# A hybrid decoder block on one core: four changes of issue order, placement and pacing in the input projection and at the start of attention

## Chip, cores and metric

The kernel runs on one core of one Trainium2 chip. The metric is the device time of one execution in microseconds (us); the time of a kernel is the median of its runs.

## The reference

One decoder block on x of 1024 tokens by 1024 channels, in float32:

```
hn   = rmsnorm(x, norm_mix)
proj = hn @ w_in          # fq fk fv ff | gq gk gv ga gb gz | gate_fox gate_gdn
y_fox = softmax(fq fk^T / sqrt(128) + cumulated log f, causal) fv        # 8 heads of 128
q, k, v = silu(causal conv of gq, gk, gv);  q, k l2-normalised
S_t = exp(g_t) (I - b_t k_t k_t^T) S_{t-1} + b_t k_t v_t^T;  o_t = S_t^T q_t   # gated delta rule
y_gdn = rmsnorm(o) * silu(gz)
h  = x + (sigmoid(gate_fox) * (y_fox @ w_branch_fox) + sigmoid(gate_gdn) * (y_gdn @ w_branch_gdn)) @ w_out
up = causal conv of (rmsnorm(h, norm_ffn) @ w_up)
out = rmsnorm(h + (silu(up_gate) * up_val) @ w_down, norm_final)
```

## The kernel before

Every float32 operand of a large product is split into a rounded high part (a cast on ScalarE, `split`, L103) and the low rest (a subtraction on VectorE or GpSimd); a product is then three matmuls: high by high, high by low, low by high. The instructions of TensorE stand in the order in which the program writes them. Those of the other engines and of the SP queue, which issues the transfers, are ordered by a scheduler that estimates when each is ready. `keep_in_program_order` pins an instruction behind the one that the program wrote before it on the same engine; later ones may still be put ahead of it.

The stages that the change touches:

**head_in (L554), 0 to about 127 us.** Tokens come in eight row tiles. For each, `norm_rows` normalises it, `columns` transposes it on TensorE and splits it into the blocks 11, 21, 12 and 22 (two halves of the channels by two halves of the tokens), and `rows` multiplies a row tile with a group of token-major weights: 24 gate columns and the values, four groups (`wgroup`, L567). A group comes as four quarters through a ring `vwr` of three raw tiles; each quarter is cast (`vwh`) and subtracted (`vwl`). Group 0 runs beside the columns, one tile behind them; groups 1 to 3 follow. Between group 0 and group 1 the program writes seven small parameter loads (`parameters`, L521, all pinned), and the low parts of group 1 are pinned on VectorE. At the start TensorE multiplies ones fifteen times (L620), with results that nobody reads. During groups 1 and 2 `block_sums` (L341) builds the blocks t1 to t4, sums and differences of the four. `scalars` (L664) computes decays from the gate columns and the parameters.

**project (L745), to about 816 us.** All other columns of w_in, 40 pairs of 128, by Strassen's scheme with seven products per pair of chunks: each product is twelve matmuls (`block_product`), and within a job the blocks come in the order 21, t2, t3, t1, (11 of the next job), 22, t4. Raw weights come through a ring `wr` of three tiles; operands are prepared three ahead (`lookahead`). The variable `left` counts the matmuls that are left. Side work is taken in steps between them: sums of the branch weights, the convolutions, the inverse of the chunk matrices on VectorE, then `prepare_lead` (L1051; a step whenever left is a multiple of 20), which stores split weights for a later stage, then `fox_first` (L1120), which loads the first attention head (ql, kl, cr, vl) and splits query and key. The last sixteen chunks are the gates: `gate(e)` (L786) takes the Tanh on ScalarE (pinned) and stores the chunk (L793) from the SP queue.

**mix (L1241), to about 1076 us.** Attention of eight heads (`fox`, L1211), 26 steps for each, with two interleaved scans of the delta rule (`stream`, `scan`). A scan's inputs are loaded by `prep(h)` (L1252), all pinned on SP: sat, sx (twice), sxt, svt, skT, skt, saq, sqd. While the second half of a head is attended, the next head's query (step 0) and key (step 3) are split by casts pinned on ScalarE (L1100) and subtractions on GpSimd.

Memory is reused by pools: a tile waits until the tiles that lay there are done. The scan's tiles lie where the blocks and the weights of project lay.

Of the kernel before, what the change touches and what calls it, by code (L numbers as in the profile page):

```python
# [9 lines left out]
F32 = mybir.dt.float32  # L10
# [7 lines left out]
P = 128  # L18
# [3 lines left out]
NT = S // P  # L22
# [45 lines left out]
def finish(gen):  # L68
    for _ in gen:
        pass  # L70
# [17 lines left out]
class Block:  # L88
# [322 lines left out]
    def run(self):  # L411
# [5 lines left out]
        with ExitStack() as ctx:  # L417
# [16 lines left out]
            banks(8)  # L434
            blk = self.blocks(pool(right, "hn", side="right"), ("11", "21", "22"))
            self.st = pool(right, "stream", side="right")
# [117 lines left out]
    def head_in(self, blk, right):  # L554
# [3 lines left out]
        with tc.tile_pool(name="hin", bufs=1) as pool, ExitStack() as px:  # L558
# [7 lines left out]

            def wgroup(g, eng):  # L567
                wh = pool.tile([P, KD * VGW], F32R, tag="vwh", bufs=2, name="vwh")
                wl = pool.tile([P, KD * VGW], F32R, tag="vwl", bufs=2, name="vwl")
                for q in range(4):  # L570
                    sl = slice(q * 2 * VGW, (q + 1) * 2 * VGW)
                    wr = pool.tile([P, 2 * VGW], F32, tag="vwr", bufs=3, name="vwr")
                    nc.sync.dma_start(wr, a["w_tok"][g][:, sl])
                    nc.scalar.copy(wh[:, sl], wr)
                    low = eng.tensor_tensor(wl[:, sl], wr, wh[:, sl].bitcast(F32), ALU.subtract)
                    if g == 1:

                        tc.keep_in_program_order(low)
                return wh, wl

# [37 lines left out]

            ps = self.small()
            for _ in range(15):  # L620
                nc.tensor.matmul(ps[:, 0:P], self.ones, self.ones, start=True, stop=True)
            xs = []
# [10 lines left out]
            for t in range(NT):  # L633
                xn = self.norm_rows(xs[t], xp, "x")
                if t == 0:
                    w0 = wgroup(0, nc.vector)
                if t + 2 < NT:
                    xload()
                columns(xn, t)
                if t:  # L640
                    rows(0, t - 1, *w0)
            rows(0, NT - 1, *w0)
            finish(params)
            px.close()
            blk.update(self.blocks(right.enter_context(tc.tile_pool(name="hnt", bufs=1, side="right", reuse_waits="tile")),
                                   ("t1", "t2", "t3", "t4")))
            scalars = self.scalars()
            for g in range(1, NVG):
                w = wgroup(g, nc.vector if g == 1 else nc.gpsimd)
                take(scalars, 1)  # L650
                for t in range(NT):
                    rows(g, t, *w)
                    if (g, t) == (2, 0):

                        self.pin = True
                        self.early = [self.wload(a["w_gdn"][i * H]) for i in range(2)]
                        self.pin = False
                    if t % 4 == 2 and g < 3:
                        sl = slice((2 * (g - 1) + t // 4) * P, (2 * (g - 1) + t // 4 + 1) * P)
                        self.block_sums(blk, whole("12", sl), whole("22", sl), sl, pool, pin=True)  # L660
# [84 lines left out]
    def project(self, blk, fox_pool):  # L745
# [40 lines left out]
        def gate(e):  # L786
            def gen(_, c):
                for _ in range(3):
                    yield
                for sl in halves[::-1]:  # L790

                    tc.keep_in_program_order(nc.scalar.activation(c[:, sl], c[:, sl], AF.Tanh, scale=0.5))
                nc.sync.dma_start(self.gt_d[e], c)  # L793
                yield
# [115 lines left out]
        with ExitStack() as ix:  # L910
            for i, _ in enumerate(self.strassen(jobs, blk, pace=3)):
# [32 lines left out]
                elif fox is None:  # L944
                    if left % 20 == 0 and not take(prep, 1):
                        ix.close()
                        ws.close()
                        fox = self.fox_first(fox_pool())
                        take(fox, 1)
                elif left in (192, 168) or left < 120 and left % 12 == 0:  # L950
                    take(fox, 1)
# [259 lines left out]
    def fox(self, pools, scan_pool):  # L1211
# [6 lines left out]
        for h in range(H):  # L1218
# [5 lines left out]
            for half in range(2):  # L1224
                for i, _ in enumerate(self.attend(h, half, pts)):
# [5 lines left out]
                    elif h + 1 < H:  # L1231
                        if i == 0:
                            self.fox_query()
                        elif i == 3:
                            self.fox_key()
# [5 lines left out]
    def mix(self, fp, pool, before_last):  # L1241
        tc, nc, a = self.tc, self.nc, self.a
        self.yf_d, self.yg_d = ([self.dr.tile([P, S], F32, name=f"{n}{h}") for h in range(H)] for n in ("yfd", "ygd"))
        if True:
# [6 lines left out]

            def prep(h):  # L1252
                def ld(tag, src, bufs=3):
                    t = pool.tile([P, NB, P], F32, tag=tag, bufs=bufs, name=tag)
                    load(t, view(src))
                    return t
                at = pool.tile([Q, NB, Q], F32, tag="sat", bufs=1, name="sat")
                load(at, self.a21_d[h])
                x11 = pool.tile([Q, NB, Q], F32, tag="sx1", bufs=1, name="sx1")
                load(x11, self.x_d[:, h * NB:(h + 1) * NB])  # L1260
                x22 = pool.tile([Q, NB, Q], F32, tag="sx2", bufs=1, name="sx2")
                y22 = self.y_d[:, Q + h * NB:Q + (h + 1) * NB]
                load(x22, y22)
                xt = pool.tile([P, NB, P], F32, tag="sxt", bufs=3, name="sxt")
                nc.gpsimd.memset(xt[Q:P, :, 0:Q], 0.0)
                load(xt[0:Q, :, 0:Q], self.y_d[:, h * NB:(h + 1) * NB])
                load(xt[Q:P, :, Q:P], y22)
                vb = ld("svt", self.vt_d[h])
# [739 lines left out]
```

## Time and profile before

| | |
|---|---|
| median of 3 runs | 2010.86 us (2009.41 to 2011.02) |
| the profiled execution | 2003.4 us, its span 2001.7 us |
| TensorE busy | 1920.6 us (96%) |
| VectorE busy | 1485.8 us (74%) |
| ScalarE busy | 1069.3 us (53%) |
| GpSimd busy | 956.5 us (48%) |
| granted TensorE clock, mean | 0.989 |

The profile names the engines PE (TensorE), DVE (VectorE), ACT (ScalarE), POOL (GpSimd) and SPq (the SP queue, which issues transfers). Times are microseconds from the start of the span. In a timeline a row has its start, its length, the engine, the line of the code, the operation, what it writes and reads, and how many instructions are merged; in brackets stands the idle time before it with the instruction that ended it. A wait for several semaphores is put down to the one that came last by the profile.

### The profile page before, as it was taken

How to read it: one execution, taken by the hardware profiler on the slowest of the kernel's cores; microseconds unless marked ns; L12 is line 12 of the kernel's file. 1: busy time of each engine (PE TensorE's matmuls, PEld its weight loads, DVE VectorE, ACT ScalarE, POOL GpSimd, SP SyncE). 2: the span in 40 equal slices, each digit the busy share in tenths (PEclk: the TensorE clock that was granted, in tenths of full speed). 3: DMA queues.
4: the chain of work that ended last, by engine and by line, in shares of the span. 5: the costliest groups of instructions: out<-in, count | busy, mean ns of one | idle time of the engine just before them, and what ended most of it. 6: DMA issues, size and time to landing. Idle time of an engine off the chain costs nothing. (4 is left out here: it accounts for less than half of the span.)

```text
span 2001.7 us, 29195 instructions
## 1 busy us (share of the span) xinstructions
PE 1920.6 (96%) x9658; PEld 1606.0 (80%) x9658; DVE 1485.8 (74%) x2549; ACT 1069.3 (53%) x2383; POOL 956.5 (48%) x792
## 2 busy tenths in 40 slices
PE   8999999999999999899998999999999999999998
PEld 8988888888887887688886887877788888878886
DVE  6848888866999974487877797668877776768435
ACT  5336777763334445476666454476555555553234
POOL 2845655655545555455655043154665656630012
PEclk9999999999999999899999999999999999999999
DMA  4324655566333366766656643573433434378654
GB/s 146 97 97 162 196 182 188 173 210 210 119 108 110 112 223 244 243 225 205 236 188 231 223 150 133 179 244 130 163 122 115 146 118 137 125 246 311 212 195 158
DMA packets 191608, 350.89 MB, mean 175 GB/s; under 512 B 50784, under 2 KB 79712, under 8 KB 191456
## 3 DMA queue, kind: packets, MB, share of 16 engines
q1 hardware_dynamic: 191312, 348.50, 51.8%
q8 instruction: 76, 1.25, 0.3%
q14 instruction: 76, 0.62, 0.1%
q10 hardware_dynamic: 144, 0.52, 0.1%
HBM read 232.76 MB, written 116.20 MB: 174 GB/s over the span
## 5 line engine op out<-in xcount | busy, mean ns | idle before, releaser
L107 POOL TENSOR_TENSOR ol<-ws,oh 128x512 fp32r<-128x512 f32 x212 | 291.2, 1376 | 217.3 <-ACT oh L106 210.9
L107 POOL TENSOR_TENSOR ol<-wr,oh 128x512 fp32r<-128x512 f32 x165 | 230.8, 1401 | 272.4 <-ACT oh L106 222.3
L106 ACT CAST oh<-ws 128x512 fp32r<-128x512 f32 x212 | 131.1, 618 | 180.6 <-PE mm L159 172.9
L205 DVE TENSOR_TENSOR ws<-wr 128x512 f32<-128x512 f32 x106 | 105.2, 992 | 103.6 <-DMA wr<-in_w_up_dram 74.3
L106 ACT CAST oh<-wr 128x512 fp32r<-128x512 f32 x201 | 121.5, 615 | 111.1 <-PE mm L159 73.5
L390 DVE SCALAR_TENSOR_TENSOR cv<-c,fw,cv 128x512 f32<-128x512 f32 (+2 forms) x176 | 127.5, 748 | 11.0 <-ACT cv L385 9.3
L390 DVE SCALAR_TENSOR_TENSOR cv<-c,cw,cv 128x511 f32<-128x511 f32 (+2 forms) x144 | 105.9, 748 | 7.4 <-ACT cv L385 5.8
L1003 DVE TENSOR_TENSOR invt<-invz 128x399 f32<-128x399 f32 (+50 forms) x114 | 94.9, 847 | 0.3
L264 ACT COPY x<-mm 128x512 f32<-128x512 f32 x158 | 91.9, 581 | 4.5 <-PE mm L159 4.5
L159 PE MATMUL mm<-b22h,oh 128*128 128x512 f32 x216 | 85.9, 398 | 5.2 <-ACT x L264 4.8
L107 DVE TENSOR_TENSOR ol<-wd,oh 128x512 fp32r<-128x512 f32 x66 | 46.4, 706 | 58.7 <-ACT oh L106 58.7
L159 PE MATMUL mm<-bt4h,oh 128*128 128x512 f32 x216 | 85.3, 395 | 3.3 <-DVE c L311 3.3
L159 PE MATMUL mm<-bt1h,oh 128*128 128x512 f32 x216 | 85.0, 393 | 3.4 <-ACT x L264 3.3
L159 PE MATMUL mm<-b11h,oh 128*128 128x512 f32 x216 | 85.5, 396 | 1.0 <-ACT oh L106 1.0
L159 PE MATMUL mm<-bt4l,oh 128*128 128x512 f32 x216 | 86.2, 399 | 0.0
L159 PE MATMUL mm<-b22l,oh 128*128 128x512 f32 x216 | 86.0, 398 | 0.0
L159 PE MATMUL mm<-b21l,oh 128*128 128x512 f32 x216 | 86.0, 398 | 0.0
L159 PE MATMUL mm<-b11h,ol 128*128 128x512 f32 x216 | 85.3, 395 | 0.7 <-POOL ol L107 0.7
L159 PE MATMUL mm<-b11l,oh 128*128 128x512 f32 x216 | 85.7, 397 | 0.0
L159 PE MATMUL mm<-bt2l,oh 128*128 128x512 f32 x216 | 85.2, 394 | 0.3 <-DVE bt2l L107 0.3
L159 PE MATMUL mm<-bt2h,oh 128*128 128x512 f32 x216 | 84.5, 391 | 1.0 <-ACT x L264 1.0
L159 PE MATMUL mm<-bt1l,oh 128*128 128x512 f32 x216 | 84.9, 393 | 0.0
(426 smaller groups left out, 6372.2 us busy)
## 6 DMA issues: line engine op xcount, KB each, us to landing
wr<-in_w_up_dram SPq DMA_DIRECT2D x43, 512.0 KB, 3.6
wr<-in_w_gdn_dram SPq DMA_DIRECT2D x24, 512.0 KB, 3.7
wr<-in_w_out_dram SPq DMA_DIRECT2D x24, 512.0 KB, 3.5
s<-hy SPq DMA_DIRECT2D x44, 256.0 KB, 3.1
s<-z SPq DMA_DIRECT2D x44, 256.0 KB, 3.3
wd<-in_w_down_dram SPq DMA_DIRECT2D x44, 256.0 KB, 5.4
b22h<-s SPq DMA_DIRECT2D x44, 256.0 KB, 3.0
b22l<-s SPq DMA_DIRECT2D x44, 256.0 KB, 3.4
```

The costliest lines, as they stand in the source:

```text
L106: cast = nc.scalar.copy(hi, src)
L107: (lo_eng or nc.vector).tensor_tensor(lo, src, hi.bitcast(F32), ALU.subtract)
L159: self.nc.tensor.matmul(ps, lhs[:, sl], rhs[:, k, :], start=(first and k == 0 and i == 0), stop=(k == 3 and i == 2), skip_group_check=True)
L205: v.tensor_tensor(t, x, y, op)
L264: nc.scalar.copy(t, x)
L390: nc.vector.scalar_tensor_tensor(t[:, lo:], c[:, 512 * j + lo - s:512 * (j + 1) - s], w[:, n - 1 - s:n - s], t[:, lo:], op0=ALU.mult, op1= ...
L1003: nc.vector.tensor_tensor(tv, z[:, m:n, 0:n].to_broadcast([P, r, n]), z[:, m, c0:c1].unsqueeze(2).to_broadcast([P, r, n]), ALU.mult))
```

## The change

Gate stores from e = 10 on are issued from ScalarE's queue. `prep(0)` no longer pins its loads; those of later heads stay pinned. The block t4 moves from the pool "hnt" into the pool "hn", and the others are placed in the order t2, t3, t1. `wgroup` becomes a generator: the ring has four raw tiles, group 0 takes its last quarter after the first `columns` (pinned), and group 1's loads and casts are written after row tile 5 of group 0, pinned, with the parameters behind them; its low parts stay where they were. Eight more products of ones follow the first `columns`. The steps of `prepare_lead` come at multiples of 16, the first query and key are split at 180 and 156 matmuls left, and within a head the next query and key are split one step later (1 and 4).

```diff
-            blk = self.blocks(pool(right, "hn", side="right"), ("11", "21", "22"))
+            blk = self.blocks(pool(right, "hn", side="right"), ("11", "21", "22", "t4"))
...
             def wgroup(g, eng):
...
-                for q in range(4):
-                    sl = slice(q * 2 * VGW, (q + 1) * 2 * VGW)
-                    wr = pool.tile([P, 2 * VGW], F32, tag="vwr", bufs=3, name="vwr")
-                    nc.sync.dma_start(wr, a["w_tok"][g][:, sl])
-                    nc.scalar.copy(wh[:, sl], wr)
-                    low = eng.tensor_tensor(wl[:, sl], wr, wh[:, sl].bitcast(F32), ALU.subtract)
-                    if g == 1:
-                        tc.keep_in_program_order(low)
-                return wh, wl
+                raw, cuts = [], [slice(q * 2 * VGW, (q + 1) * 2 * VGW) for q in range(4)]
+                def high(q, pin):
+                    raw.append(pool.tile([P, 2 * VGW], F32, tag="vwr", bufs=4, name="vwr"))
+                    load = nc.sync.dma_start(raw[q], a["w_tok"][g][:, cuts[q]])
+                    cast = nc.scalar.copy(wh[:, cuts[q]], raw[q])
+                    if pin:
+                        tc.keep_in_program_order(load)
+                        tc.keep_in_program_order(cast)
+                def low(q, pin):
+                    ins = eng.tensor_tensor(wl[:, cuts[q]], raw[q], wh[:, cuts[q]].bitcast(F32), ALU.subtract)
+                    if pin:
+                        tc.keep_in_program_order(ins)
+                for q in range(3 if g == 0 else 4):
+                    high(q, g == 1)
+                    if g == 0:
+                        low(q, False)
+                yield wh, wl
+                if g == 0:
+                    high(3, True)
+                    low(3, False)
+                else:
+                    for q in range(4):
+                        low(q, g == 1)
...
-            ps = self.small()
-            for _ in range(15):
-                nc.tensor.matmul(ps[:, 0:P], self.ones, self.ones, start=True, stop=True)
+            def warm(n):
+                ps = self.small()
+                for _ in range(n):
+                    nc.tensor.matmul(ps[:, 0:P], self.ones, self.ones, start=True, stop=True)
+            warm(15)
...
                 if t == 0:
-                    w0 = wgroup(0, nc.vector)
+                    group = wgroup(0, nc.vector)
+                    w0 = next(group)
                 if t + 2 < NT:
                     xload()
                 columns(xn, t)
                 if t:
                     rows(0, t - 1, *w0)
+                else:
+                    finish(group)
+                    warm(8)
+                if t == NT - 2:
+                    group = wgroup(1, nc.vector)
+                    w1 = next(group)
+                    finish(params)
             rows(0, NT - 1, *w0)
-            finish(params)
             px.close()
             blk.update(self.blocks(right.enter_context(tc.tile_pool(name="hnt", bufs=1, side="right", reuse_waits="tile")),
-                                   ("t1", "t2", "t3", "t4")))
+                                   ("t2", "t3", "t1")))
             scalars = self.scalars()
             for g in range(1, NVG):
-                w = wgroup(g, nc.vector if g == 1 else nc.gpsimd)
+                if g > 1:
+                    group = wgroup(g, nc.gpsimd)
+                    w1 = next(group)
+                w = w1
+                finish(group)
                 take(scalars, 1)
...
-                nc.sync.dma_start(self.gt_d[e], c)
+                (nc.scalar if e >= 10 else nc.sync).dma_start(self.gt_d[e], c)
...
-                    if left % 20 == 0 and not take(prep, 1):
+                    if left % 16 == 0 and not take(prep, 1):
...
-                elif left in (192, 168) or left < 120 and left % 12 == 0:
+                elif left in (180, 156) or left < 120 and left % 12 == 0:
...
-                        if i == 0:
+                        if i == 1:
                             self.fox_query()
-                        elif i == 3:
+                        elif i == 4:
                             self.fox_key()
...
             def prep(h):
+                def load_input(dst, src):
+                    if h:
+                        load(dst, src)
+                    else:
+                        nc.sync.dma_start(dst, src)
...
-                    load(t, view(src))
+                    load_input(t, view(src))
...
-                load(at, self.a21_d[h])
+                load_input(at, self.a21_d[h])
...
```

The loads of x11, x22 and xt change in the same way.

## Rows read from the trace of the kernel before

**Rows 1.** Timeline of TensorE in head_in: dummy products and three waits.

```profile
1.19 5.49 PE L621 MATMUL ms<-ones 128*128 128x128 f32 x30 [1.19 <-POOL ones L509]
...
10.42 1.10 PE L605 MATMUL ms<-ident,nxn 128*128 128x128 f32 x8 [1.99 <-DVE nxn L551]
...
53.85 0.59 PE L587 MATMUL ms<-vwh,b21h 128*128 128x262 f32 x1 [5.95 <-ACT vwh L574]
...
105.34 0.39 PE L588 MATMUL ms<-vwl,b21h 128*128 128x262 f32 x1 [0.70 <-POOL vwl L575]
```

**Rows 2.** Timelines of ScalarE, SP and VectorE at the border of groups 0 and 1.

```profile
37.77 0.37 ACT L591 COPY vev<-ms 128x262 f32<-128x262 f32 x1
...
45.09 0.43 SPq L526 DMA_DIRECT2D nf<-in_norm_ffn_dram  x1
...
48.47 7.86 SPq L573 DMA_DIRECT2D vwr<-in_w_tok_dram  x5
...
49.11 0.31 DVE L686 SCALAR_TENSOR_TENSOR z<-sm,fb 128x64 f32<-128x64 f32 x1 [1.68 <-DMA fb<-in_fox_f_bias_dram]
```

**Rows 3.** Stretches at a lowered clock: length, busy of PE, PEld, DVE, ACT, POOL; clock, DMA, GB/s.

```profile
12.85:19.09 6.24, 6.24 (x30) 6.24 (x31) 5.39 (x10) 3.73 (x8) 1.89 (x3) 0.52 0.88 277
53.85:59.81 5.96, 5.52 (x23) 5.22 (x24) 5.82 (x9) 3.04 (x6) 3.31 (x3) 0.50 0.52 146
...
786.73:790.25 3.52, 3.52 (x10) 2.86 (x10) 0.90 (x5) 0.49 (x2) 2.23 (x2) 0.52 0.03 5
820.00:829.00 9.00, 6.84 (x50) 5.52 (x49) 7.85 (x25) 4.95 (x12) 1.89 (x3) 0.81 1.06 348
838.36:843.00 4.64, 4.64 (x30) 3.90 (x31) 2.53 (x5) 3.11 (x8) 4.30 (x5) 0.67 1.09 319
```

**Rows 4.** Timeline of TensorE, 780 to 840: its four waits of over 1 us.

```profile
784.17 0.38 PE L1152 MATMUL ms<-kh,qh 128*128 128x256 f32 x1 [1.54 <-ACT kh L1100]
786.73 0.54 PE L1153 MATMUL ms<-kl,qh 128*128 128x256 f32 x1 [2.17 <-POOL kl L1101]
...
823.45 1.19 PE L1283 MATMUL ms<-sx,sat 64*64 64x64 f32 x16 [2.16 <-DVE mm L1167]
...
838.36 0.79 PE L1316 MATMUL us<-su,saq 128*128 128x128 f32 x2 [6.76 <-DMA sx<-yd]
```

**Rows 5.** SP queue: longest wait in 770 to 816 (total, times, longest); three issues.

```profile
SPq L793 <- ACT c L792: 29.9, 5, 22.0
...
773.69 0.42 SPq L1084 DMA_DIRECT2D ql<-qd  x1
...
815.45 0.50 SPq L1250 DMA_DIRECT2D sat<-a21d  x1
...
825.94 0.32 SPq L1084 DMA_DIRECT2D ql<-qd  x1
```

**Rows 6.** Timeline of ScalarE at 837.

```profile
837.00 1.14 ACT L1100 CAST qh<-ql 128x512 fp32r<-128x512 f32 x2 [5.83 <-DMA ql<-qd]
838.05 0.26 ACT L1311 COPY su<-us 128x128 f32<-128x128 f32 x1
```

**Rows 7.** Three stretches around the start of attention (columns as in rows 3).

```profile
775.00:815.00 40.00, 35.61 (x151) 28.73 (x150) 12.11 (x35) 16.23 (x34) 19.76 (x18) 0.96 0.31 104
815.00:845.00 30.00, 20.96 (x138) 17.66 (x137) 16.99 (x50) 14.28 (x32) 14.04 (x12) 0.83 1.04 340
725.00:775.00 50.00, 49.02 (x217) 40.08 (x216) 28.88 (x36) 29.79 (x54) 25.62 (x18) 1.00 0.97 345
```

**Rows 8.** The page's DMA issues: count, size, us from issue to landing.

```profile
wr<-in_w_gate_dram SPq DMA_DIRECT2D x16, 512.0 KB, 3.8
```

**Rows 9.** Timelines of GpSimd and TensorE in mix: a switch of heads, a late ql.

```profile
907.90 2.53 POOL L1101 TENSOR_TENSOR kl<-kl,kh 128x512 fp32r<-128x512 f32 x2
...
911.09 0.28 PE L1153 MATMUL ms<-kl,qh 128*128 128x256 f32 x1
...
1000.43 0.49 PE L1315 MATMUL us<-ss,sqd 128*128 128x128 f32 x2 [1.87 <-ACT su L1311]
```

More of the change, by code (lines that the diff above doesn't have):

```diff
@@ L1252, in prep @@
             def prep(h):
+                def load_input(dst, src):
[3 more added lines that the diff above has]
+                        nc.sync.dma_start(dst, src)
                 def ld(tag, src, bufs=3):
                     t = pool.tile([P, NB, P], F32, tag=tag, bufs=bufs, name=tag)
-                    load(t, view(src))
+                    load_input(t, view(src))
                     return t
                 at = pool.tile([Q, NB, Q], F32, tag="sat", bufs=1, name="sat")
-                load(at, self.a21_d[h])
+                load_input(at, self.a21_d[h])
                 x11 = pool.tile([Q, NB, Q], F32, tag="sx1", bufs=1, name="sx1")
-                load(x11, self.x_d[:, h * NB:(h + 1) * NB])
+                load_input(x11, self.x_d[:, h * NB:(h + 1) * NB])
                 x22 = pool.tile([Q, NB, Q], F32, tag="sx2", bufs=1, name="sx2")
                 y22 = self.y_d[:, Q + h * NB:Q + (h + 1) * NB]
-                load(x22, y22)
+                load_input(x22, y22)
                 xt = pool.tile([P, NB, P], F32, tag="sxt", bufs=3, name="sxt")
                 nc.gpsimd.memset(xt[Q:P, :, 0:Q], 0.0)
-                load(xt[0:Q, :, 0:Q], self.y_d[:, h * NB:(h + 1) * NB])
-                load(xt[Q:P, :, Q:P], y22)
+                load_input(xt[0:Q, :, 0:Q], self.y_d[:, h * NB:(h + 1) * NB])
+                load_input(xt[Q:P, :, Q:P], y22)
                 vb = ld("svt", self.vt_d[h])
```

## The prediction

> **What bounds the kernel now.** TensorE is busy nearly all the time (table above) and its instructions stand in an order written out by hand, so the time is its work plus its idle stretches plus what a lowered clock costs. I read the waits of TensorE first, then the timeline around each long wait on TensorE and on the engine named as releaser, then the SP queue there, and last the granted clock and DMA share of those stretches. Four places stand out, and the change touches all of them.
>
> At the border between the first and the second weight group TensorE idles 5.95 us, released by a cast of weights [rows 1]. It had to wait, since the last quarter of the second group's weights was issued at 48.47 only, behind seven parameter loads that begin at 45.09 and behind a free slot in a ring of three [rows 2]. Afterwards the clock stands at 0.50, its lower level of 1.2 GHz, for 5.96 us [rows 3]. I price a slow stretch as (1 - clock) x length, the time that the work would not have needed at 2.4 GHz: here 2.98 us.
>
> At the start of attention two score products wait 1.54 and 2.17 us for operands of the first head [rows 4]; ql, their source, was issued at 773.69 [rows 5]. The clock is at 0.52 for the next 3.52 us: 1.69 us more [rows 3].
>
> Then 2.16 us before the products of the first scan's preparation [rows 4]. The row names VectorE, but their operand sat was issued at 815.45 [rows 5], 8 us before that, so I read it as a transfer. 9 us at 0.81 cost 1.7 us [rows 3].
>
> The longest wait is 6.76 us at 838.36 [rows 4]. It is put down to a load, but sx was used long before. TensorE restarts when ScalarE has copied su at 838.05, and this copy stood behind the casts qh<-ql, which waited 5.83 us for the transfer of ql [rows 6]. That ql was issued at 825.94 [rows 5], in 30 us with the DMA engines at a share of 1.04 [rows 7]. 4.64 us at 0.67 follow: 1.5 us [rows 3].
>
> **The change, part by part.** The sum is made against the profiled execution, 2003.4 us.
>
> (a) Second group. Its four loads now precede the parameters and are pinned behind the store of row tile 5; with four slots none waits for a subtraction. Tile 5 is evicted at 37.77 [rows 2], so the loads go out from about 38; with some 0.4 us for each issue and the 4 us that weights take to land [rows 8] the four are in SBUF near 43.5, and the first of them is cast before the group begins at about 44. The low parts stay pinned behind the last sm copy, so the short wait at the very border stays. Gone: 5.95 + 2.98 = 8.9 us, of which a second wait inside the slow stretch is a part. What is late next: the scalars, which began at 49.11 with the landing of fb [rows 2], and the block sums after them on VectorE and GpSimd. The parameters now come earlier, but four subtractions and the last sm copy still come first, so I let this chain gain 3 us where TensorE gains 9. In group 3 TensorE already waits 0.70 us for GpSimd's low parts [rows 1]. What is given back is thus between 0 and 8.9 - 3 = 5.9; I take 1.5, since only the last quarter was late there and the ring now has a fourth slot. Queued behind the new loads on SP are the parameters and the store of tile 6, neither urgent. Queued behind the new casts on ScalarE can be the casts of row tile 7; the pin alone does not force that, so I take 0, with a bound of +4.5 (held from 39 until the loads land near 43.5). Net **-7.4** (-8.9 to +1.5).
>
> (b) Eight dummy products between the first and second column step. They fall into the 1.99 us in which TensorE waits for nxn [rows 1]. Fifteen cost 5.49 us [rows 1], at the lower rate, so eight cost 2.9 there and half at the higher: +0.9 to nothing. If they keep the clock up, they save up to 0.48 x 6.24 = 3.0 us [rows 3], but VectorE, which prepares the next row tile, was busy for 5.39 of these 6.24 us [rows 3], so all beyond 0.85 us would turn into a wait for it. The last quarter of the first group's weights has its slot from the start. I take **-1.0** (-3.0 to +0.9).
>
> (c) Gate stores on ScalarE's queue, lead steps every 16 products, first queries at 180 and 156 left. SP stands 29.9 us for the Tanh of gates in 770 to 816, once 22.0 us [rows 5]. The two gate stores that it issues just ahead of 773.69 leave SP. The inverse ends at 360 products left; seven lead steps then fall at 352 down to 256 instead of 340 down to 220, so the first head's tiles open 36 products sooner in the program, at 0.23 us each (49.02 us for 217 [rows 7]) 8 us. Against that, DMA is at 0.97 through 725 to 775 [rows 7], so the lead stores may not finish much sooner. The chain must come about 4 us earlier to empty the wait. Of 3.71 + 1.69 = 5.4 us I take **-4.0** (-5.4 to 0). On ScalarE the stores cost an issue each, as on SP (0.42 us [rows 5]): four of the six fall into idle time; the last two stand ahead of the value casts and exponentials of the first head, +0.8 at most; **+0.4**.
>
> (d) First scan's loads. Unpinned, and with t2, t3 and t1 placed where sat, sx, sxt and svt will lie, and t4 away from them, they can start as those blocks end (the last job runs 21, t2, t3, t1, 22, t4, twelve products of 0.23 us each): the four blocks behind t2 take 11 us, so from about 804 instead of 815.45. The DMA share of 775 to 815 is 0.31 [rows 7]. That clears the 2.16 + 1.7 and takes some 3 MB out of the crowded 30 us [rows 7], so the next ql need not take the 11 us from its issue to its cast; and this cast comes one attention step later. Behind these loads on SP stand the loads of w_out, not used for 400 us. Of 3.9 + 8.3 = 12.2 us I take **-10.5** (-12.2 to -2), since the second scan's loads are still pinned behind ql and share the same stretch.
>
> (e) The same later step in heads 2 to 7. At 1000.43 TensorE waits 1.87 us for su behind a ql that is not there yet [rows 9]: most of it goes. In the second switch of heads kl ends at 910.43 and is used at 911.09, a slack of 0.66 us [rows 9] against a step of about 1.25 (eight heads of 26 steps in some 260 us): +0.6. **-0.7** (-1.9 to +4, if GpSimd is late at each switch).
>
> (f) The fourth vwr slot moves the tiles behind it by 2.1 KB, so the projection's first operands reuse other bytes, perhaps the last evictions'. Nothing in the trace shows it; between 0 and the 2 us of a last store, taken **+0.5**.
>
> Sum: -7.4 - 1.0 - 4.0 + 0.4 - 10.5 - 0.7 + 0.5 = -22.7. From 2003.4 that is 1980.7. The median of the runs stands 7.46 us above the profiled execution; I assume the same after: **1988 us**.
>
> **The rivals.** (1) *The DMA engines, not the queues, set the landings.* In 725 to 775 and again in 815 to 845 their share is 0.97 and 1.04 [rows 7]. If ql lands no sooner in either place or if the scheduler leaves the unpinned loads behind SP's other work (the change then doesn't do what it says), (c) and most of the last wait, 4 + 7 us, are lost: 1999. Against it: between the two stretches the engines are at 0.31 while SP stands still [rows 5, 7]. The Trainium skill (DMA: Bandwidth & Descriptors, Issuing engines are not separate DMA queues) says that transfers from several issuing engines share the same 16 DMA engines and that spreading them saves only issue time. By that rule alone (c) would give nothing and the time would be 1992; the 22 us that SP stood behind one store is a wait in the queue that the rule does not count.
>
> (2) *GpSimd becomes the bound of group 3*, giving back 5.9 instead of 1.5: 1992. For it speaks the 0.70 us it already costs [rows 1].
>
> (3) *Slower: the denser lead steps starve the weights.* 36 products' worth of lead traffic moves into 50 us with no DMA share left [rows 7]. Gate weights land 3.8 us after issue [rows 8]; three operands of twelve products lie ahead, 3 x 2.7 = 8.2 us, so a landing beyond 12 us stops TensorE. If each of the last four jobs waited 6 us and paid 1.5 us of clock, that is +30, and (c) is lost: 1988 + 30 + 4 = 2022. It decides from about 12 us of landing; now it is a third of that, which speaks against it.
>
> **How the numbers follow.** Forecast 0.62, rival 1 0.18, rival 2 0.11, rival 3 0.09. The forecast's own range is 1980 (all bounds of gain) to 1997; rivals 1 and 2 reach 1999 with their own spread to 2004. Below 1980 and above 2004 I leave 2 in 10. A measurement of this kernel can tell 0.2%, 4 us, from no change. Faster, below 2006.8: most of the first three cases, 0.84; the same 0.07, from rival 1 together with the bad bounds of (a); slower 0.09, from rival 3.
>
> **What would show it.** Right: no wait of 5.95 us at the border of the groups and a clock of 1.0 after it; gate stores on ScalarE's queue and no wait of 22 us on SP; sat issued near 804; no ScalarE wait of over 2 us for ql before the first su copies. Wrong: ql issued as late as now, group 3 waiting several us for vwl, ScalarE holding the casts of tile 7, or weights late in the last jobs of the projection.

## The result, and the profile after

The changed kernel takes 1996.91 us (median of 4 runs, 1993.43 to 2000.16) where the kernel before takes 2010.43: a ratio of 0.9933, 95% interval 0.9911 to 0.9955. Measured a second time, beside the last variant below, it takes 1992.96 us (1990.97 to 1994.50), ratio 0.9905 (0.9886 to 0.9925). Faster, as forecast, inside the range of 1980 to 2004, but 5 to 9 us short of the forecast 1988.

One pair of profiles does not give the size. The profiled execution of before (2003.4 us) was one of its shortest: its runs in all comparisons lie between 2002.15 and 2016.38. So both kernels were profiled twice. The table follows TensorE from landmark to landmark (start of the row in its timeline; second head: its first `kh,qh` product after the second `sx,sat`):

| stretch of TensorE | before | before, again | after | after, again | mean change | forecast |
|---|---|---|---|---|---|---|
| start to first product of project | 127.71 | 130.20 | 119.74 | 118.70 | -9.7 | -7.9 (a, b, f) |
| from there to the second head | 722.51 | 724.64 | 723.24 | 722.20 | -0.9 | -14.1 (c, d) |
| second head to the merge | 227.25 | 231.09 | 224.72 | 224.64 | -4.5 | -0.7 (e) |
| merge to the end of the span | 924.2 | 926.5 | 924.9 | 924.3 | -0.8 | 0 |
| span | 2001.7 | 2012.4 | 1992.6 | 1989.8 | -15.9 | -22.7 |

So the total is near the forecast because the first and third rows gave more than was asked of them, while the parts that carried most of the forecast gave almost nothing. The second row hides two halves, which the first score product (the first `kh,qh` row) divides. Up to it the stretch takes 656.46 and 657.85 us before and 660.03 and 660.05 after, 2.9 us more; from it to the second head 66.05 and 66.79 before and 63.21 and 62.15 after, 3.7 us less. What the profile after shows at each place:

At the border of the weight groups the four loads go out in one piece behind the store of tile 5. SP timeline of the changed kernel (start, length):

```profile
38.17 1.87 SPq L576 DMA_DIRECT2D vwr<-in_w_tok_dram  x4
40.08 0.43 SPq L527 DMA_DIRECT2D nf<-in_norm_ffn_dram  x1
```

and its TensorE timeline there and in the first scan:

```profile
46.30 0.39 PE L608 MATMUL ms<-vwl,b11h 128*128 128x262 f32 x1 [2.34 <-DVE vwl L583]
...
49.73 0.42 PE L607 MATMUL ms<-vwh,b21h 128*128 128x262 f32 x1
...
782.82 0.39 PE L1188 MATMUL ms<-kl,qh 128*128 128x256 f32 x1 [2.77 <-POOL kl L1136]
...
819.30 0.55 PE L1224 MATMUL ms<-ident,p 128*128 128x128 f32 x3 [0.83 <-DVE mx L1194]
820.90 0.41 PE L1224 MATMUL ms<-ident,p 128*128 128x128 f32 x2 [1.06 <-DVE mx L1194]
822.24 0.48 PE L1224 MATMUL ms<-ident,p 128*128 128x128 f32 x1 [0.93 <-DVE pl L107]
...
834.36 1.11 PE L1325 MATMUL ms<-sx,sat 64*64 64x64 f32 x16 [0.91 <-DMA sx<-xd]
```

Of [rows 1] the 5.95 us and the 0.70 us of group 3 are gone; the short wait at the border has grown from 1.21 to 2.34. Of [rows 4] the 1.54, the 2.16 and the 6.76 us are gone, 2.17 has become 2.77, and four short waits are new. Busy time, clock and DMA share of the stretches (columns as in [rows 3]):

```profile
44.00:53.80 9.80, 7.50 (x49) 7.50 (x50) 7.64 (x15) 5.37 (x12) 3.68 (x4) 0.83 0.50 155
53.80:59.80 6.00, 6.00 (x51) 6.00 (x51) 5.79 (x9) 1.96 (x5) 3.92 (x3) 1.00 0.72 219
...
775.00:815.00 40.00, 36.55 (x160) 29.91 (x158) 12.00 (x42) 18.99 (x38) 18.86 (x18) 0.96 0.34 112
815.00:845.00 30.00, 26.03 (x175) 22.01 (x175) 17.95 (x54) 14.67 (x37) 16.87 (x15) 0.83 0.98 332
...
821.70:831.90 10.20, 9.55 (x44) 8.19 (x45) 4.58 (x9) 4.13 (x10) 0.72 (x1) 0.50 1.03 387
```

The 6 us behind the border run at full clock now. The clock is not whole there, though: behind the 2.34 us it is low, and 0.83 over the 9.8 us of the first row is 1.7 us lost by the prediction's own pricing, so of its 2.98 us some 1.3 are won. The last row follows three waits that sum to 2.82 us: 10.2 us at 1.2 GHz, 5.1 us lost, where the two slow stretches of [rows 3] in 820 to 843 cost 1.7 + 1.5.

By the clock of the trace the transfers came sooner. SP timeline of the changed kernel around attention:

```profile
766.91 0.32 SPq L1100 DMA_DIRECT2D lead<-parts  x1
767.28 1.19 SPq L1119 DMA_DIRECT2D ql<-qd  x1
...
800.23 0.50 SPq L1293 DMA_DIRECT2D sat<-a21d  x1
...
814.03 0.33 SPq L1293 DMA_DIRECT2D skT<-kTd  x1
...
816.99 1.65 SPq L126 DMA_DIRECT2D wr<-in_w_out_dram  x3
818.74 0.45 SPq L1119 DMA_DIRECT2D kl<-kd  x1
819.93 0.33 SPq L1119 DMA_DIRECT2D ql<-qd  x1
821.18 0.32 SPq L1148 DMA_DIRECT2D cr<-rows  x1
822.47 0.47 SPq L1285 DMA_DIRECT2D sat<-a21d  x1
```

Against [rows 5] the first ql leaves 6.4 us earlier, where TensorE itself is 4.4 us earlier (779.77 against 784.17); sat 15.2 us; the second ql 6.0 us, which is no more than TensorE's lead there (6.1 us at the first `sx,sat`). The first ql is no sooner either when it is counted from the projection's first product: 645.98 and 647.37 us behind it in the two traces of before, 647.54 and 647.45 in the two of after. Its 6.4 us are the lead that the border gave. The gate stores are gone from in front of it, but SP issues it right behind the last lead store. The longest waits of SP between 770 and 816 (total, times, longest) name what holds the rest:

```profile
SPq L1293 <- PE mm L159: 25.6, 1, 25.6
SPq L1293 <- DMA gtd<-c: 10.0, 1, 10.0
```

The first is the wait for the blocks to end; the second is new: skT waits 10 us for a gate store, which suggests that it lies where that store's chunk lay, and w_out, the second head and the second scan stand behind skT on SP.

### The profile page after: what moved, and what is told of

It is laid out like the page before. It is cut to its first block, busy times and chain, and to the rows that moved or that the text cites. A ratio compares the mean times of both kernels' runs of the same rounds, so it can differ in the third digit from the quotient of the medians.

```text
span 1992.6 us, 29214 instructions
## 1 busy us (share of the span) xinstructions
PE 1920.6 (96%) x9674; PEld 1605.2 (81%) x9674; DVE 1492.4 (75%) x2549; ACT 1067.5 (54%) x2383; POOL 954.3 (48%) x792
## 5 line engine op out<-in xcount | busy, mean ns | idle before, releaser
L205 DVE TENSOR_TENSOR ws<-wr 128x512 f32<-128x512 f32 x106 | 99.1, 935 | 103.2 <-DMA wr<-in_w_up_dram 70.5
L159 PE MATMUL mm<-b21h,oh 128*128 128x512 f32 x216 | 84.9, 393 | 0.0
```

Source lines behind the costliest of these rows:

```text
L159: self.nc.tensor.matmul(ps, lhs[:, sl], rhs[:, k, :], start=(first and k == 0 and i == 0), stop=(k == 3 and i == 2), skip_group_check=True)
L205: v.tensor_tensor(t, x, y, op)
```

## The experiments

All times are medians in us. The last three columns are the stretches of the table above, from one profiled execution of each; two executions of one kernel differ there by up to 2.5, 2.1 and 3.8 us (table above). "Ratio" is to the kernel before on the same chip.

| kernel | median (runs) | ratio, interval | project starts | to second head | to merge |
|---|---|---|---|---|---|
| no_dummies | 1994.64 (4) | 0.9930, 0.9906 to 0.9955 | 120.36 | 722.40 | 223.27 |
| gates_old | 2004.37 (10) | 0.9977, 0.9962 to 0.9992 | 118.63 | 733.63 | 222.99 |
| scan_old | 1995.67 (4) | 0.9930, 0.9911 to 0.9950 | 118.02 | 722.20 | 227.31 |
| steps_old | 1999.34 (6) | 0.9949, 0.9922 to 0.9975 | 118.55 | 721.54 | 228.37 |
| gates_only | 2010.20 (10) | 0.9990, 0.9977 to 1.0002 | 128.64 | 726.11 | 226.58 |
| gates_sp | 1998.26 (4) | 0.9943, 0.9926 to 0.9961 | 119.08 | 729.80 | 222.51 |
| pace_old | 2001.56 (6) | 0.9950, 0.9930 to 0.9970 | 117.86 | 731.13 | 225.05 |
| group2_only | 1998.81 (4) | 0.9940, 0.9925 to 0.9954 | 119.62 | 724.42 | 228.84 |
| steps_only | 2007.35 (10) | 0.9985, 0.9967 to 1.0002 | 130.26 | 726.98 | 223.21 |
| first_key | 1992.17 (4) | 0.9902, 0.9882 to 0.9923 | 119.11 | 721.59 | 223.39 |

**no_dummies.** The changed kernel less this:

```diff
                 else:
                     finish(group)
-                    warm(8)
```

> The changed kernel without the eight extra dummy products. Theory (the dummies only trade a lowered clock at the first column steps for a wait for VectorE): the clock is at its lower level again for 6 to 7 us near 12 to 19, TensorE's waits there shrink by the same amount, the first product of the input projection stays at 119.7 +- 0.7 us and the time stays within 3 us of the changed kernel. Rival (the kept clock is part of the 8 us that are gained before the projection): the projection starts 1.5 to 3.4 us later and the time is 1.5 to 3.4 us longer.

The clock is low again (6.80 us at 0.50). TensorE timeline and one stretch of no_dummies:

```profile
10.65 1.09 PE L625 MATMUL ms<-ident,nxn 128*128 128x128 f32 x8 [2.27 <-DVE nxn L552]
```

```profile
11.90:18.70 6.80, 5.71 (x27) 5.62 (x27) 6.15 (x11) 3.74 (x7) 3.08 (x4) 0.50 0.49 158
```

VectorE is busy 6.15 of these 6.8 us, and 6.36 of the same 6.8 us in the changed kernel, where the clock is 1.00: I read it as what sets the pace at either clock. The projection starts at 120.36, 119.62 in group2_only, also without dummies; with them, in eight traces, at 117.86 to 119.74. About 1 us, and none of it shows in the median. The theory holds as to the start and the time. That the dummies alone keep the clock up is not shown: group2_only has 1.00 in the same 6.8 us without them.

**group2_only.** The kernel before with the new `wgroup` and its place alone (that part of the diff above).

> The kernel before, with the second weight group's part alone: ring of four, loads and casts ahead of the parameters; no dummies, old blocks, stores, pace, loads and steps. Theory: the projection starts 8 us sooner, at 119.7 +- 1, of this 4 to 6 us are left at the first score product because the small waits of the projection fall otherwise, and the waits of 1.5, 2.2, 2.2 and 6.8 us around 784 to 838 stay; the time is 4 to 8 us shorter. Rival (the lead is worth nothing since the chain of ql and sat sets the start of attention): the waits at 784 to 838 grow by what was gained and the time is within 2 us of the kernel before.

The projection starts at 119.62, 9.6 us ahead of the mean of four traces without this part (127.71, 130.20, 128.64, 130.26; 8.1 ahead of the first, on which the sum was made), and the stretch behind it is as long as before: nothing is given back. So the theory was right on the place and too small on the time, since I had let 2 to 4 us be lost on the way to attention: 0.9940 is 12 us. The waits around 784 to 838 stay; the longest is 5.81 us, for a copy of su behind casts that wait for ql, as before. ScalarE timeline of group2_only:

```profile
830.11 1.14 ACT L1134 CAST qh<-ql 128x512 fp32r<-128x512 f32 x2 [4.88 <-DMA ql<-qd]
831.15 0.26 ACT L1348 COPY su<-us 128x128 f32<-128x128 f32 x1
```

The ratio of this one part, 0.9940, is nearly that of the whole change (0.9933 and 0.9905).

**gates_old, gates_sp, pace_old.** The changed kernel with (c) undone: both edits, the queue alone, the pace alone.

```diff
-(nc.scalar if e >= 10 else nc.sync).dma_start(self.gt_d[e], c)
+nc.sync.dma_start(self.gt_d[e], c)
...
-if left % 16 == 0 and not take(prep, 1):
+if left % 20 == 0 and not take(prep, 1):
...
-elif left in (180, 156) or left < 120 and left % 12 == 0:
+elif left in (192, 168) or left < 120 and left % 12 == 0:
```

> The changed kernel with the gate stores back on the SP queue, lead steps every 20 products and the first query and key at 192 and 168. Theory (the earlier transfer of ql and kl is lost in the queue of ScalarE and in GpSimd's two subtractions, and the denser lead steps cost small waits in the last jobs): ql is issued 4 to 8 us later again, but the first score product comes within 1.5 us of its place in the changed kernel (779.8), the waits for x and c in 640 to 760 shrink by 1 to 2 us, and the time stays within 2 us. Rival (the prediction's term of 4.0 is there and hidden by something else): the two waits of 1.5 and 2.2 us come back, with a lowered clock behind them, and the time is 4 us longer.

> The changed kernel with the gate stores on the SP queue alone; lead steps at 16 and queries at 180 and 156 stay. Theory (the queue is what counts): SP stands behind a store in 796 to 813 again, the wait of about 5 us before the second preparation near 840 is there as in the kernel with both put back, and the second head starts 8 to 10 us later than in the changed kernel. Rival (the pace is what counts): ql of the second head is issued within 2 us of 820 and the time stays within 2 us of the changed kernel.

> The changed kernel with lead steps every 20 products and queries at 192 and 168; the gate stores stay on ScalarE's queue. Theory: the pace counts for little, the first score product comes within 2 us of 779.8, the second head within 2 us, and the time within 2 us of the changed kernel. Rival (the denser steps bring the first ql): ql is issued 4 us later, the first score product waits 3 us more and the time is 3 to 5 us longer.

All three lengthen the middle stretch, by 10.9, 7.1 and 8.4 us against the mean of after (722.7). My theory for gates_old was wrong (its rival asked for less than came, and at another place). The one for gates_sp held in its mechanism, with 7.1 us for the 8 to 10 that it named: SP stands in front of the gate stores, and TensorE pays at the second scan. SP and TensorE timelines of gates_sp:

```profile
782.14 29.05 SPq L828 DMA_DIRECT2D gtd<-c  x4
...
826.06 0.47 SPq L1285 DMA_DIRECT2D sat<-a21d  x1
...
837.13 1.84 PE L1325 MATMUL ms<-sx,sat 64*64 64x64 f32 x16 [5.12 <-DMA sx<-xd]
```

The first row is four stores merged, from the issue of the first to the end of the last. What SP waited there, in 770 to 816 (total, times, longest):

```profile
SPq L828 <- ACT c L826: 37.5, 5, 12.9
```

In pace_old ql leaves as early as in the changed kernel (765.75, 647.89 us behind the projection's first product), and still 1.54 and 2.17 us are waited before the first scores. ScalarE timelines, first of pace_old:

```profile
778.97 1.14 ACT L1135 CAST qh<-ql 128x512 fp32r<-128x512 f32 x2
781.16 0.62 ACT L106 CAST oh<-wr 128x512 fp32r<-128x512 f32 x1 [1.06 <-PE mm L159]
...
782.16 1.14 ACT L1135 CAST kh<-kl 128x512 fp32r<-128x512 f32 x2
```

then of the changed kernel:

```profile
777.08 0.62 ACT L106 CAST oh<-wr 128x512 fp32r<-128x512 f32 x1 [1.61 <-PE mm L159]
777.61 1.14 ACT L1135 CAST qh<-ql 128x512 fp32r<-128x512 f32 x2
778.65 1.14 ACT L1135 CAST kh<-kl 128x512 fp32r<-128x512 f32 x2
```

With kl landed (issued 766.68, 8.2 us to land in that trace), the key's cast of pace_old waits in ScalarE's queue behind a weight cast that waits for TensorE; with the new steps it stands right behind the query's. The kernel before shows the same. ScalarE timeline of before:

```profile
782.50 0.62 ACT L106 CAST oh<-wr 128x512 fp32r<-128x512 f32 x1 [1.07 <-PE mm L159]
783.02 0.58 ACT L264 COPY x<-mm 128x512 f32<-128x512 f32 x1
783.50 1.14 ACT L1100 CAST kh<-kl 128x512 fp32r<-128x512 f32 x2
```

kl was issued at 774.16 and took 7.0 us to land, so it lay ready at 781.2, and its cast began at 783.50. The wait of 1.54 us stands in all seven traces with the old pace and in none of the seven with the new one. So the pace matters, against my theory, by the order on ScalarE, and not by the transfer, as the rival had it. Its full 8 us are not explained: 5 of them lie before the first score product, most in small waits for x that vary between traces (see below).

**gates_only.** The kernel before with the first line of that diff alone, turned round.

> The kernel before, with nothing changed but the gate stores from e = 10 on, which go out from ScalarE's queue. Theory (the stores that waited for the Tanh on SP held back the loads of the second head, and this is where the second half of the gain comes from): ql and kl of the second head are issued 4 to 8 us sooner than 825, the wait of 6.76 us for su shrinks to under 3 us, the second head starts 5 to 9 us sooner than in the kernel before and the time is 4 to 9 us shorter. Rival (the loads' place and the pins matter as well, so that the stores alone give little): w_out and sat are issued no sooner than 811, a wait of over 5 us stays near 838, and the time is within 2 us.

No difference that can be told (0.9990), and the rival held: w_out leaves at 817.63, sat at 818.95, 8.4 us ahead of its first product as before (8.0), and 6.17 us are waited for su. The pinned loads follow w_out directly, with the stores or without; it is not the stores that hold them up here. The Trainium skill (DMA: Bandwidth & Descriptors, Issuing engines are not separate DMA queues) says that moving a transfer to another engine saves only the time of issuing it. This run agrees; gates_sp does not: there the move is worth 7 us in the trace, since SP waits 37.5 us in all in front of the stores and everything behind them waits too.

**scan_old.** The changed kernel with all loads of `prep(h)` pinned and the blocks in their old pools and order.

```diff
...
-                    if h:
-                        load(dst, src)
-                    else:
-                        nc.sync.dma_start(dst, src)
+                    load(dst, src)
```

> The changed kernel with the first scan's loads pinned again and the blocks in their old order and pools. Theory (of the predicted 10.5 us the earlier loads give about 3, since where TensorE no longer waits for sat it waits for the softmax of VectorE and ScalarE instead): sat is issued 8 to 15 us later, the wait of about 2 us before the first L1321 products returns, the four short waits behind it go, and the first product of the second head is 2 to 4 us later. Rival (the prediction's term): the long wait of 5 to 7 us for su behind the cast of ql returns too, and the second head is 8 to 12 us later.

No difference up to the second head: 722.20, as in the changed kernel, median 1995.67. The 2.6 us more from there to the merge stand beside 3.4 us lost at a lowered clock near 957, which I can't tie to the edit. sat leaves at 806.89, 9.7 us ahead of its first product (17.1 in the changed kernel, 8.0 in the kernel before). TensorE timeline of scan_old:

```profile
816.61 1.73 PE L1321 MATMUL ms<-sx,sat 64*64 64x64 f32 x16 [3.03 <-DVE p L1203]
...
831.59 1.11 PE L1321 MATMUL ms<-sx,sat 64*64 64x64 f32 x16 [2.24 <-DMA sx<-xd]
```

One wait of 3.03 us in place of three that sum to 2.82, 5.1 us lost at 1.2 GHz behind it as behind those, and then the second scan's loads. The theory had the waits right and still asked 2 to 4 us too much of part (d).

**steps_old, steps_only.** Steps 0 and 3 in the changed kernel; steps 1 and 4 in the kernel before.

```diff
-                        if i == 1:
+                        if i == 0:
...
-                        elif i == 4:
+                        elif i == 3:
```

> The changed kernel with query and key split at steps 0 and 3 again. Theory (the long wait of 6.76 us went because the next ql is issued 6 us earlier and lands near 830.6, not because its cast comes one step later): no wait over 2 us in 825 to 850; the wait of 1.9 us for su behind ql near 992 returns, with its lowered clock, so 1.5 to 3.6 us are lost there and nowhere else. Rival (the later step is what removed it): a wait of 3 to 6 us for su returns near 831 and the second head starts 3 to 6 us later.

> The kernel before with the next head's query and key split one step later, and nothing else. Theory (the wait of 6.76 us is one of order: ScalarE's copy of su stands behind the cast qh, which waits for ql): the copy of su now stands ahead of the cast and the wait of 6.76 us is gone; in its place TensorE waits 2 to 5 us for sat and sx of the second scan, whose loads are pinned behind ql, so that 2 to 5 us are gained at the first switch, and 2 to 3 us more where 1.87 us were waited near 1000. Rival (it is the late ql itself): a wait of over 5 us for su stays, and the second head starts no sooner.

steps_old: no long wait in 825 to 850, and 2.34 us near 993, as expected, with 3.7 us more from the second head to the merge. There the scheduler has put the casts of ql and kl behind the copy of su by itself, so this run does not tell an earlier ql from a later cast; steps_only does. ScalarE and TensorE timelines of steps_only:

```profile
835.33 0.28 ACT L1311 COPY su<-us 128x128 f32<-128x128 f32 x1
...
842.03 1.14 ACT L1100 CAST qh<-ql 128x512 fp32r<-128x512 f32 x2 [5.92 <-DMA ql<-qd]
```

```profile
837.29 0.46 PE L1316 MATMUL us<-su,saq 128*128 128x128 f32 x2 [1.43 <-DMA saq<-aqd]
845.42 1.94 PE L1283 MATMUL ms<-sx,sat 64*64 64x64 f32 x16 [6.31 <-DMA sx<-xd]
```

ql is as late as ever, su no longer waits for it, and TensorE stops 8 us further on for 6.31 us, for the second scan's loads. At the first switch nothing is gained, where the theory asked for 2 to 5 us. Further on it is: 223.21 us from the second head to the merge against 227.25 and 231.09.

**first_key.** The changed kernel with one more edit, meant to beat it.

```diff
...
         self.fox_query()
         yield
-        self.fox_key()
+        self.fox_key(self.nc.vector)
```

> The changed kernel with one more edit: the low part of the first head's key is subtracted on VectorE instead of GpSimd, where it stands behind the 2.5 us of the query's. Theory: the wait of 2.77 us before the second score product goes (under 0.8 us stays), with it the lowered clock behind it, 1.7 us, and half or all of this is left at the end: 2 to 4 us less than the changed kernel. Rival (TensorE runs into the softmax of VectorE sooner, as it did in the first scan): the waits for mx and pl near 820 grow by as much and the time is within 1 us of the changed kernel.

The wait fell from 2.77 to 0.86, and the time hardly moved: 1992.17 against 1992.96 on the same chip, four runs each, so that a gain of 2 us is not ruled out. From the first score product to the second head it takes 62.24 us, 62.15 in after_again on that chip. The rival held as to the time, but not in the way it said: the waits for the softmax and then for `sx<-xd` (0.84, 1.06, 0.85, 0.40, 1.50) sum to 4.65, as in after_again (4.57; 3.73 in the first trace of after). What came in place of most of the 1.9 us is a lowered clock behind the 1.50. The stretch from the second scan's first product to the second head, in first_key and in after_again (columns as in [rows 3]):

```profile
830.50:840.70 10.20, 10.18 (x75) 9.01 (x75) 3.48 (x7) 2.98 (x8) 9.67 (x9) 0.83 0.72 265
832.28:840.90 8.62, 8.62 (x74) 7.63 (x75) 3.35 (x7) 2.81 (x7) 7.76 (x8) 1.00 0.87 319
```

**before_again, after_again.** Both kernels, profiled once more.

> The kernel before, unchanged, profiled once more. Theory (its first profiled execution, 2003.4 us, was one of its shortest, since the runs of it lie between 2002 and 2016 with a median near 2011, so that the comparison of the two profiles shows some 5 us less than the medians do): this execution takes 2006 to 2014 us, the large waits stand where they stood, and the difference lies in more or longer stretches of the lower clock (each costs about half its length) and in small waits for x and c in the projection. Rival (the profile costs or saves time itself): it takes 2003 us again and shows the same stretches.

> The changed kernel, unchanged, beside the run with the key on VectorE on the same chip. Expected: a median of 1994 to 1999 us, the waits of 2.8 us before the second score product and of about 3 us in all for the softmax near 820, and no long wait in 825 to 850.

Timelines of before_again, first TensorE, then ScalarE:

```profile
23.30 0.39 PE L587 MATMUL ms<-vwh,b11h 128*128 128x262 f32 x1 [1.86 <-ACT b11h L106]
...
1007.62 0.79 PE L1315 MATMUL us<-ss,sqd 128*128 128x128 f32 x2 [4.06 <-ACT su L1311]
```

```profile
1006.27 1.14 ACT L1100 CAST qh<-ql 128x512 fp32r<-128x512 f32 x2 [4.02 <-DMA ql<-qd]
```

2014.12 us, just past the far end of what the theory said. The wait of 1.87 us of [rows 9] is 4.06 us here with 6.9 us of lowered clock behind it: what the later step removes is twice as dear in this execution as in the one on which I priced it. after_again shows the waits of after, one of them (`sx<-xd`) 2.14 instead of 0.91; its median is 1 us below what I expected.

## Why the prediction was right, and where it failed

**Right by the sum, not by its terms.** The forecast of "faster" rested on four places. The border paid; the three at the start of attention together gave 0.9 us of 14.1. That the sum came out within 5 to 9 us is in part luck: the first stretch gave 1.8 us and the heads after the second 3.8 us more than they were asked for, and nothing in the prediction says why they should.

**(a) right, undersized.** The mechanism is as told: loads out from 38.17 and no wait of 5.95. 9.6 us instead of 7.4 (8.1 against the execution on which the sum was made). "What is given back ... I take 1.5" was the wrong step: no wait at group 3, GpSimd is not late (rival 2 falls). Two things are worse than told: the short wait at the border grew from 1.21 to 2.34, and the clock is low behind it (1.7 us), where the prediction had all 2.98 us gone.

**(b)** About 1 us at the projection's start, as taken, lost in the scatter of the runs. **(f)** not to be seen.

**(c) and (d): the failed steps.** "Of 3.71 + 1.69 = 5.4 us I take -4.0" and "Of 3.9 + 8.3 = 12.2 us I take -10.5". Together 14.5 less 0.4; measured 0.9. I took each wait as bounded by a transfer and asked only whether the transfer came sooner. For (c) both halves were wrong. That "the first head's tiles open 36 products sooner" did not bring ql forward: it landed 5.3 us sooner (767.28 + 7.3 against 773.69 + 6.2), but the projection began 8.0 us sooner. And ql's transfer was not what the first scores waited for, even before: kl lay ready 2.3 us before its cast, which stood behind a weight cast on ScalarE. What ends the wait now is two query subtractions on GpSimd in front of the key's.

For (d) sat did leave 15 us sooner, 9 of them against TensorE. What I did not ask is what ends the stage then. In the first scan it is the softmax on VectorE and ScalarE, then the second scan's loads behind skT, w_out and ql on one SP queue with the DMA engines at 0.98. scan_old brings the later sat back and waits as much in one piece; steps_only takes the wait of 6.76 us away and waits 6.31 us for the next loads; first_key saves 1.9 us and loses most of them at a lowered clock. The long wait itself was a matter of order: the copy of su behind a cast that waits.

Of the 13.2 us by which these terms fell short, 2.9 lie in front of the first score product and are not explained (see the end of this section). Behind it 3.7 us were gained. Neither edit of (d) carries them alone: from the first score product to the second head scan_old takes 62.68 us without the earlier loads and steps_old 61.95 without the later step. How sure they are is open too, since no_dummies takes 66.42 with both, with 3.4 us lost at a lowered clock behind its second scan's first product.

What (c) does is keep the rest from getting worse: without it the stretch is 7 to 11 us longer (gates_sp, gates_old; in the medians 1 to 5, within the scatter, and 7 to 11, beyond it), its stores alone give nothing (gates_only). The parts do not add up, and a sum of parts was my method.

**(e) right, undersized.** "-0.7" against 4.5. The clock behind the 1.87 us was left out of this term, the give-back at the key (+0.6) did not come, and the execution I read showed the smallest wait of the five with the old steps (1.87; 1.89 in group2_only, 2.34 in steps_old, 2.53 in gates_only, 4.06 in before_again). None of the nine traces with the new steps waits over 0.4 us there.

**The rivals.** Rival 1 came nearest to what happened to (c) and (d), more by its number than by its mechanism: of 14 us some 13 were lost, ql came no sooner against the projection, and the second scan's loads are late while the DMA share is 0.98. But the unpinned loads did leave early, and at the first scores it was the order on ScalarE and not the landing. Its 1999 is 2 to 6 us too long because (a) and (e) gave more. Rival 3's starved weights never came: no wait of TensorE for weights of over 1 us in the last jobs.

**Still open.** Between the start of the projection and the first score product the traces with this change take 656 to 665 us, those without 656 to 660, with waits for ScalarE's x and VectorE's c, none over 2.7 us, that fall otherwise in every trace. The waits for x of over 0.3 us sum to 4.3 to 5.3 us in the kernel before and with one part alone, and to 5.9 to 11.1 in the changed kernel and its variants, so the parts together seem to cost some 3 us there. I could tie them to no single edit. Loading w_out later, to free 1.5 MB in the crowded stretch, was not tried.

## What to carry to other kernels

Before pricing a wait as gained, name what would end the stage if it were gone, and take the time up to that, not the wait. Where several waits stand within 50 us of each other on one path, undo and do each part alone: here the stores and the later step left the stretch 2.5 and 3.4 us longer when done alone (two traces of the kernel before differ by 2.1), all parts together shortened it by 0.9, and without the stores' part it grew by 7 to 11. A releaser's row names who ended a wait; what that engine had in its own queue just before says why it came so late. And price from two profiled executions at least: one that lies at the edge of the runs misprices the waits that vary most.

## What the runs showed of the hardware

A VectorE operation on two 128x512 tiles, 0.69 us at its shortest, took 1.56 and 1.78 us for the subtraction of kl in first_key, where GpSimd subtracted ql at the same time (2.98 us for two, against 2.52). It is not the only one: the block sums `tt<-tw,tt`, with GpSimd at work beside them, take 1.59 to 1.86 us in the changed kernel, while operations that read one operand from a product's result (`c<-mm,x`) stay at 0.67 to 0.69 beside GpSimd too. VectorE timeline of first_key, the pair merged:

```profile
777.98 3.26 DVE L1136 TENSOR_TENSOR kl<-kl,kh 128x512 fp32r<-128x512 f32 x2 [1.87 <-ACT kh L1135]
```

The Trainium skill (SBUF — State Buffer, SBUF: two separate sides) says that the two engines take a shared port in turn, each for a whole instruction, when VectorE reads two operands from SBUF, the on-chip memory of the tiles, and GpSimd reads there too; a wait of 0.9 to 1.1 us for the other's 1.27 fits that. And three short waits of under 1.1 us each, 2.82 in all, were followed by 10.2 us at 1.2 GHz in which TensorE was busy for 9.55: the clock cost more than the waits. In after_again a wait of 2.77 us before the second score product was followed by no lowered clock, in the first trace of after by 1.7 us lost.
